# A product moved to the last step of each seven-product unit, and three products given a PSUM bank of their own, in a two-layer decoder kernel

## The chip, the cores and the metric

The kernel runs on one core of one Trainium2 chip. The metric is the device time of one execution in microseconds (us), lower is better. Below, PE is TensorE (matmuls), ACT is ScalarE, DVE is VectorE, POOL is GpSimd and SP is SyncE; SP and POOL issue the DMA transfers.

## The reference

A trunk of two layers on a sequence of 256 tokens with 2048 channels, all in float32. Layer 0 has differential attention, layer 1 latent attention, and each is followed by a SwiGLU feed-forward network (FFN). The change lies in the two FFNs alone:

```python
def _swiglu(h, w_in, w_out):
    g, u = jnp.split(h @ w_in, [FFN_HIDDEN], axis=-1)
    return (jax.nn.silu(g) * u) @ w_out

# in each layer i, FFN_HIDDEN = 5632
y = _swiglu(_rmsnorm(x, g[2]), ffn_w_in[i], ffn_w_out[i])
x = x + _rmsnorm(y, g[3])
```

## The kernel before

**Split matmuls.** Every float32 operand is split into a high and a low part (`split_to`: ACT makes the high part by a cast, L105, then DVE the low part by a subtraction, L106). A product of two such operands is three matmuls (`mm3`, L100 to L102). A piece of weights is 128 x 4 x 512 numbers, 1 MB. It comes by DMA into a staging buffer (`wst`, 2 buffers, or `wr`, 3 buffers) and is split in two halves into `whi` and `wlo`, which hold 6 halves each, three pieces. A product of one piece with one block of tokens is 12 matmuls of 512 columns.

**Blocks.** The hidden width is worked through in 11 blocks of 512 (`blk` 0 to 10). A block's input part makes the gate (m = 0) and the up half (m = 1) for the two blocks of 128 tokens (t = 0, 1) in four sums of the pool `mm` (4 PSUM banks). Odd blocks and blocks 0 and 10 do it in the plain way (`block_in`, 8 pieces of 24 matmuls). Blocks 2, 4, 6 and 8, the even blocks here, do half of it by seven products in place of eight, after Strassen and Winograd (`block_in_sevens`): seven products of 12 matmuls and four plain pieces of 24.

**Units.** The output part of two finished blocks is made by `unit`, again by seven products, from four pieces of `wout`. While an odd block from 3 on is worked on, two units run between its pieces, and block 10 has one: 9 units in each FFN. A unit's sums are in the pool `wp` (2 banks); each product's share is added to `y` in SBUF by `gather` (DVE, L716; or ACT, L713, where nothing is there yet).

**The right factors.** The seven right factors of a unit or an even block are sums of four weight pieces b11, b12, b21, b22, made in place in the three `wr` buffers by `right_factors`. Before, step k splits: 0 b11; 1 b21; 2 b11 + b12; 3 b22; 4 b11 + b12 + b22; 5 b12 + b22, the third sum; 6 the sum of all four. Two sums are made by DMAs that POOL issues and that add b12 from DRAM to a buffer: L690, after step 0's split, for step 2; and L694, after step 3's split and after the DVE addition L693, for step 5. The other two are DVE additions, L693 (for step 4) and L696 (for step 6).

**The even block's banks.** In `block_in_sevens` the bank `a` (the gate's sum for t = 1) holds step 0, then steps 4 and 5 on top of it, then step 6 and two plain pieces. Step 2 is alone in a `wp` bank (`lone`). DVE reads `a` after steps 4 (L600) and 5 (L604).

**Order.** Dependences, buffers and the order on each engine come from a planner that simulates the program; each engine then runs its list in that order, and so do the DMA queues' issuers SP and POOL. After block 8, `x_again` (L790) has POOL load the kept residual, 2 MB, into the buffer that the even blocks' left factors (`S`) held till then.

Of the kernel before, what the change touches and what calls it, by code (L numbers as in the profile page):

```python
# [9 lines left out]
F32 = mybir.dt.float32  # L10
# [4 lines left out]
ALU = mybir.AluOpType  # L15
AX = mybir.AxisListType

P = 128
SEQ = 256
NT = SEQ // P  # L20
D = 2048
KC = D // P
CW = 512
# [16 lines left out]
def trunk_kernel(ctx: ExitStack, tc: tile.TileContext, a: dict):  # L40
    nc = tc.nc
# [10 lines left out]
    sb = ctx.enter_context(tc.tile_pool(name="sb", bufs=2))  # L52
# [20 lines left out]
    def load_split(src, shape, loads=1, parts=1):  # L73

        w = wst.tile([P] + shape, F32, tag="w", name="w")
        n = shape[0] // loads
        for i in range(loads):
            nc.sync.dma_start(w[:, i * n : (i + 1) * n], src[:, i * n : (i + 1) * n])  # L80
        return split_weight(w, shape, parts)

    def split_weight(w, shape, parts=1):
        both = []
        half = shape[0] // 2
        for h in range(2):
            hi = whi.tile([P, half] + shape[1:], F32R, tag="whi", name="whi")
            lo = wlo.tile([P, half] + shape[1:], F32R, tag="wlo", name="wlo")
            n = half // parts
            for i in range(parts):  # L90
                c = slice(i * n, (i + 1) * n)
                split_to(hi[:, c], lo[:, c], w[:, h * half + i * n : h * half + (i + 1) * n])
            both += [(hi[:, i], lo[:, i]) for i in range(half)]
        return both
# [232 lines left out]
    def x_piece(ps, piece, kcs, t, first=None, more=False):  # L327
        first = kcs[0] == 0 if first is None else first
        for k, kc in enumerate(kcs):
            ts_ = slice(t * P, (t + 1) * P)  # L330
            mm3(ps, (xTh[:, kc, ts_], xTl[:, kc, ts_]), piece[k], first and k == 0, kc == KC - 1, more)
# [131 lines left out]
    def ffn(i, rstd, second_tokens, first_tokens, aside=None):  # L463
        win, wout = a[f"win{i}"], a[f"wout{i}"]
# [5 lines left out]
        def activation(g, u, hidden):  # L470
            hs = []
            for t in range(NT):
                sg = sb.tile([P, CW], F32, tag="t2k", bufs=4, name="sg")
                nc.scalar.activation(sg, g(t), AF.Silu, scale=rows[t])
                h = sb.tile([P, CW], F32, tag="t2k", bufs=4, name="h")
                nc.vector.scalar_tensor_tensor(h, u(t), rows[t], sg, op0=ALU.mult, op1=ALU.mult)
                hs.append(h)
            for t in (1, 0):
                pt = tr.tile([P, CW], F32, tag="tr", name="pt")
                for j in range(4):  # L480
                    nc.tensor.transpose(pt[:, j * P : (j + 1) * P], hs[t][:, j * P : (j + 1) * P], ident)
                hidden(t, pt.rearrange("p (k t) -> p k t", k=4))
# [26 lines left out]
        I = {}  # L509
# [56 lines left out]
        def block_in_sevens(blk, hidden):  # L566

            ps = {k: mm.tile([P, CW], F32, tag="mm", name="ps") for k in ((0, 1), (1, 0), (1, 1), (0, 0))}
            G = {k: gp.tile([P, CW], F32, tag="g", name="G") for k in ("11", "12", "22")}
            lone = wp.tile([P, CW], F32, tag="wp", name="lone")  # L570
            begun = set()

            def plain(m, pc, t, piece=None):
                piece = load_split(win[blk, m, pc], [4, CW]) if piece is None else piece
                x_piece(ps[m, t], piece, range(pc * 4, pc * 4 + 4), t, (m, t) not in begun, True)
                begun.add((m, t))
                return piece

            right = right_factors(win[blk, 0, 0], win[blk, 1, 0], win[blk, 0, 1], win[blk, 1, 1])

            def step(k, left, out, key=None):
                product(out, I[left], right(k), more=key in begun or k in (4, 5))
                if key:
                    begun.add(key)

            a, c = ps[0, 1], ps[1, 0]
            right(None)
            yield
            step(0, "A11", a, (0, 1))
            nc.scalar.copy(G["11"], a)  # L590
            u2 = plain(1, 2, 0)
            plain(1, 2, 1, u2)
            step(1, "A12", ps[0, 0], (0, 0))
            step(2, "-S1", lone)
            nc.scalar.copy(G["22"], lone)
            u3 = plain(1, 3, 0)
            plain(1, 3, 1, u3)
            step(3, "-S4", c, (1, 0))
            step(4, "S2", a)
            nc.vector.tensor_tensor(G["12"], G["22"], a, op=ALU.subtract)  # L600
            nc.vector.tensor_tensor(G["12"], c, G["12"], op=ALU.add)
            g2 = plain(0, 2, 0)
            step(5, "S3", a)
            nc.vector.tensor_tensor(G["22"], G["22"], a, op=ALU.subtract)  # L604
            nc.vector.tensor_tensor(G["22"], ps[1, 1], G["22"], op=ALU.add)
            g3 = plain(0, 3, 0)
            nc.vector.tensor_tensor(G["11"], ps[0, 0], G["11"], op=ALU.add)
            plain(0, 2, 1, g2)
            step(6, "A22", a, (0, 1))
            plain(0, 3, 1, g3)  # L610
            yield
            activation(lambda t: a if t else G["11"], lambda t: G["22"] if t else G["12"], hidden)

        def parts(name):
            both = mid.tile([P, 2, 2, 4, P], F32R, tag="mid", name=name)
# [53 lines left out]
        def product(ps, lhs, rhs, more=False):  # L669

            for k in range(4):
                mm3(ps, (lhs[0][:, k], lhs[1][:, k]), rhs[k], not more and k == 0, k == 3, more)

        def right_factors(b11, b12, b21, b22):

            w = {}

            def raw(src):
                t = wr.tile([P, 4, CW], F32, tag="r", name="wr")
                nc.sync.dma_start(t, src)  # L680
                return t

            def right(k):
                if k is None:
                    w["t"] = raw(b11)
                    w["b21"] = raw(b21)
                    return
                now = split_weight(w[("t", "b21", "t", "b22", "t", "b22", "t")[k]], [4, CW])
                if k == 0:
                    nc.gpsimd.dma_start(w["t"], b12, accum_op=ALU.add)  # L690
                    w["b22"] = raw(b22)
                elif k == 3:
                    nc.vector.tensor_tensor(w["t"], w["t"], w["b22"], op=ALU.add)  # L693
                    nc.gpsimd.dma_start(w["b22"], b12, accum_op=ALU.add)  # L694
                elif k == 4:
                    nc.vector.tensor_tensor(w["t"], w["t"], w["b21"], op=ALU.add)  # L696
                return now

            return right

        def unit(pair, X, cgs, first):

            (b1, b2), (n1, n2) = pair, cgs

            def sums():
                return wp.tile([P, CW], F32, tag="wp", name="wp")

            def ys(t, cg):
                return y[:, t, cg * CW : (cg + 1) * CW]

            def gather(t, cg, ps, sign, fresh=False):
                if fresh:
                    nc.scalar.mul(ys(t, cg), ps, sign)  # L713
                else:
                    op = ALU.add if sign > 0 else ALU.subtract
                    nc.vector.tensor_tensor(ys(t, cg), ys(t, cg), ps, op=op)  # L716

            right = right_factors(wout[b1, n1], wout[b1, n2], wout[b2, n1], wout[b2, n2])
            right(None)
            yield  # L720
            for k, left in enumerate(("A11", "A12", "S1", "S4", "S2", "S3", "A22")):
                if k == 0:
                    pa = sums()
                elif k in (1, 2):
                    pc = sums()
                ps, more = (pc, k == 3) if k in (1, 2, 3) else (pa, k > 0)
                product(ps, X[left], right(k), more)
                if k == 0:
                    gather(0, n1, ps, 1.0, first)
                elif k == 1:  # L730
                    gather(0, n1, ps, 1.0)
                elif k == 2:
                    gather(1, n2, ps, -1.0, first)
                elif k == 3:
                    gather(0, n2, ps, -1.0, first)
                elif k == 4:
                    gather(0, n2, ps, -1.0)
                elif k == 5:
                    gather(1, n2, ps, -1.0)
                else:  # L740
                    gather(1, n1, ps, 1.0, first)
                yield

        def chained(units):
# [49 lines left out]
        for blk in range(NBLK):  # L794
            if blk == NBLK - 1:
                A, hidden = single_operands()
                plain = plain_unit(pair, X, (2, 3))
# [392 lines left out]
```

## Time and profile before

| | |
|---|---|
| time, median of 3 runs | 2116.52 us (2114.79 to 2123.14) |
| the profiled execution | 2125.41 us, of which the span of the profile is 2123.6 us |
| busy in the span | PE 2066.8 us (97%), DVE 1606.5 (76%), ACT 1160.7 (55%), POOL 90.3 |
| granted clock of TensorE | 0.991 of full speed, mean over the span |

All times in the profile are microseconds from the first instruction unless marked ns. The ends of matmuls are modelled, so that a row's duration (0.39 us for 512 columns) is longer than the distance of two starts.

### The profile page before, as it was taken

Reading aid. Unit: us, or ns where it says so; the run is one execution under the profiler, and the core shown is the slowest. Engines: PE = TensorE matmul, PEld = TensorE weight load, DVE = VectorE, ACT = ScalarE, POOL = GpSimd, SP = SyncE. Lnnn points to the kernel's source line nnn. Section 1 sums busy time; section 2 is a strip of 40 time slices with the busy share of each in tenths; the row PEclk is TensorE's granted clock in tenths of the full one; section 3 lists DMA queues with packets and bytes.
Section 4 is the critical chain, followed back from the end, with each engine's and each line's share of the span. In section 5 each row is a group of like instructions: output and inputs, shape, how many; then the busy total and the mean of one; then the engine's idle time right before and its main releaser. Section 6 shows DMA issues by size and latency. Waiting matters only on the chain.

```text
span 2123.6 us, 26407 instructions
## 1 busy us (share of the span) xinstructions
PE 2066.8 (97%) x10278; PEld 1756.8 (83%) x10278; DVE 1606.5 (76%) x1851; ACT 1160.7 (55%) x1509; POOL 90.3 (4%) x139
## 2 busy tenths in 40 slices
PE   8999999999999999999998999999999999999997
PEld 7999998788887878878888898878777887878886
DVE  6655655777888888978777876486888888888866
ACT  6444444555665555646545654465655665556543
POOL 0000000000000000000001100000000000000000
PEclk9999999999999999999999999999999999999999
DMA  7554546466767767688644534466677776778752
GB/s 264 198 179 159 175 163 225 160 234 186 226 203 212 254 209 236 185 256 269 199 164 162 201 117 164 139 240 215 179 210 235 230 217 195 245 227 255 225 196 104
DMA packets 63772, 430.62 MB, mean 203 GB/s; under 512 B 7584, under 2 KB 7840, under 8 KB 14112
## 3 DMA queue, kind: packets, MB, share of 16 engines
q1 hardware_dynamic: 55584, 366.03, 47.2%
q0 software_dynamic: 8064, 62.92, 15.2%
q8 instruction: 80, 1.31, 0.2%
q14 instruction: 44, 0.36, 0.0%
HBM read 422.63 MB, written 6.29 MB: 202 GB/s over the span
## 4 chain that ended last, share of the span: by engine, by line
PE 75%; DVE 9%; DMA 8%; issue 6%; ACT 2%; POOL 0%; SPq 0%; ACTq 0%; POOLq 0%; DVEq 0%
PE ps L100 20%; PE ps L101 20%; PE ps L102 20%; DVE wlo L106 5%; DMA wr<-in_win 5%; PE wp L102 4%; PE wp L101 4%; PE wp L100 4%; DMA wr<-in_wout 2%; ACT whi L105 2%; DVE wr L693 1%; DVE x L260 1%; PE ps_s L1049 0%; PE ps_s L388 0%; PE ps_s L1050 0%
## 5 line engine op out<-in xcount | busy, mean ns | idle before, releaser
L106 DVE TENSOR_TENSOR wlo<-w,whi 128x1024 fp32r<-128x1024 f32 (+3 forms) x534 | 637.7, 1203 | 253.6 <-ACT whi L105 244.4
L105 ACT CAST whi<-w 128x1024 fp32r<-128x1024 f32 (+3 forms) x534 | 546.7, 1034 | 441.6 <-PE ps L102 255.9
L100 PE MATMUL ps<-whi,xTh 128*128 128x512 f32 (+2 forms) x1472 | 566.4, 391 | 19.9 <-ACT whi L105 16.6
L101 PE MATMUL ps<-wlo,xTh 128*128 128x512 f32 (+2 forms) x1472 | 570.0, 388 | 3.5 <-DVE wlo L106 3.4
L102 PE MATMUL ps<-whi,xTl 128*128 128x512 f32 (+2 forms) x1472 | 566.8, 387 | 1.4 <-DVE xTl L106 1.4
L106 DVE TENSOR_TENSOR wlo<-wr,whi 128x1024 fp32r<-128x1024 f32 x364 | 436.1, 1219 | 155.6 <-ACT whi L105 152.8
L105 ACT CAST whi<-wr 128x1024 fp32r<-128x1024 f32 x364 | 374.8, 1049 | 311.7 <-PE ps L102 107.2
L100 PEld LDWEIGHTS ps<-whi,xTh 128*128 128x128 f32 x1472 | 277.5, 189 | 78.3 <-ACT whi L105 20.5
L101 PEld LDWEIGHTS ps<-wlo,xTh 128*128 128x128 f32 x1472 | 278.1, 189 | 59.0 <-DVE wlo L106 6.5
L102 PEld LDWEIGHTS ps<-whi,xTl 128*128 128x128 f32 x1472 | 278.0, 189 | 55.5 <-DVE xTl L106 1.7
L100 PE MATMUL ps<-xTh,whi 128*128 128x256 f32 x512 | 146.3, 287 | 0.0
L102 PE MATMUL ps<-xTh,wlo 128*128 128x256 f32 x512 | 144.9, 283 | 0.2 <-DVE wlo L106 0.2
L101 PE MATMUL ps<-xTl,whi 128*128 128x256 f32 x512 | 144.7, 283 | 0.0
L100 PE MATMUL ps<-whi,oTh 128*128 128x512 f32 x256 | 100.7, 393 | 0.0
L101 PE MATMUL ps<-wlo,oTh 128*128 128x512 f32 x256 | 100.0, 391 | 0.0
L102 PE MATMUL ps<-whi,oTl 128*128 128x512 f32 x256 | 99.9, 390 | 0.0
L102 PEld LDWEIGHTS ps<-xTh,wlo 128*128 128x128 f32 x512 | 98.2, 192 | 0.5 <-DVE wlo L106 0.4
L101 PEld LDWEIGHTS ps<-xTl,whi 128*128 128x128 f32 x512 | 98.2, 192 | 0.3
L100 PEld LDWEIGHTS ps<-xTh,whi 128*128 128x128 f32 x512 | 98.1, 192 | 0.3
L716 DVE TENSOR_TENSOR y<-y,wp 128x512 f32<-128x512 f32 x110 | 74.8, 680 | 6.1 <-PE wp L102 5.8
L696 DVE TENSOR_TENSOR wr<-wr 128x2048 f32<-128x2048 f32 x26 | 59.4, 2285 | 0.3
L693 DVE TENSOR_TENSOR wr<-wr 128x2048 f32<-128x2048 f32 x26 | 59.4, 2284 | 0.1
(276 smaller groups left out, 2785.9 us busy)
## 6 DMA issues: line engine op xcount, KB each, us to landing
w<-in_win SPq DMA_DIRECT2D x144, 1024.0 KB, 5.7
wr<-in_wout SPq DMA_DIRECT2D x54, 1024.0 KB, 5.6
wr<-in_wout POOLq DMA_DIRECT2D x36, 1024.0 KB, 8.8
w<-in_wqk SPq DMA_DIRECT2D x32, 1024.0 KB, 4.8
w<-in_wo SPq DMA_DIRECT2D x32, 1024.0 KB, 4.9
wr<-in_win SPq DMA_DIRECT2D x24, 1024.0 KB, 6.9
wr<-in_win POOLq DMA_DIRECT2D x16, 1024.0 KB, 8.4
w<-in_wout SPq DMA_DIRECT2D x16, 1024.0 KB, 4.9
```

The source lines that it names most:

```text
L100: nc.tensor.matmul(out, lh, rh, start=first, stop=False, skip_group_check=more)
L101: nc.tensor.matmul(out, lh, rl, start=False, stop=False, skip_group_check=more)
L102: nc.tensor.matmul(out, ll, rh, start=False, stop=last, skip_group_check=more)
L105: nc.scalar.copy(hi, src)
L106: nc.vector.tensor_tensor(lo, src, hi.bitcast(F32), op=ALU.subtract)
L260: nc.vector.scalar_tensor_tensor(xs, y[:, t, cg * CW : (cg + 1) * CW], ry, xs, op0=ALU.mult, op1=ALU.add)
L693: nc.vector.tensor_tensor(w["t"], w["t"], w["b22"], op=ALU.add)
L696: nc.vector.tensor_tensor(w["t"], w["t"], w["b21"], op=ALU.add)
L716: nc.vector.tensor_tensor(ys(t, cg), ys(t, cg), ps, op=op)
```

## The change

Steps 5 and 6 are exchanged in each unit and in each even block: the sum of all four weight pieces is now split for step 5 and multiplied with A22, and the third sum, b12 + b22, that L694's DMA makes, is split for step 6 and multiplied with S3. In an even block, steps 0, 4 and 6 go to a second `wp` bank, `chain`, and `ps[0, 1]` holds the plain pieces and step 5 alone; since the gate's sum for t = 1 is then in two banks, ACT copies `chain` to SBUF (`sums`) and DVE adds `ps[0, 1]`. Plain pieces are no longer divided over two places, and the second follows step 3. In a unit, step 5 has a `wp` bank to itself, and step 6 joins steps 0 and 4, from where it is added to two places of `y`: one more `gather` a unit.

```diff
@@ -567,49 +567,49 @@
 
             ps = {k: mm.tile([P, CW], F32, tag="mm", name="ps") for k in ((0, 1), (1, 0), (1, 1), (0, 0))}
             G = {k: gp.tile([P, CW], F32, tag="g", name="G") for k in ("11", "12", "22")}
-            lone = wp.tile([P, CW], F32, tag="wp", name="lone")
+            lone, chain = (wp.tile([P, CW], F32, tag="wp", name=k) for k in ("lone", "chain"))
             begun = set()
 
-            def plain(m, pc, t, piece=None):
-                piece = load_split(win[blk, m, pc], [4, CW]) if piece is None else piece
-                x_piece(ps[m, t], piece, range(pc * 4, pc * 4 + 4), t, (m, t) not in begun, True)
-                begun.add((m, t))
-                return piece
+            def plain(m, pc):
+                piece = load_split(win[blk, m, pc], [4, CW])
+                for t in range(NT):
+                    x_piece(ps[m, t], piece, range(pc * 4, pc * 4 + 4), t, (m, t) not in begun, True)
+                    begun.add((m, t))
 
             right = right_factors(win[blk, 0, 0], win[blk, 1, 0], win[blk, 0, 1], win[blk, 1, 1])
 
-            def step(k, left, out, key=None):
-                product(out, I[left], right(k), more=key in begun or k in (4, 5))
-                if key:
-                    begun.add(key)
-
-            a, c = ps[0, 1], ps[1, 0]
+            def step(k, left, out):
+
+                if isinstance(out, tuple):
+                    product(ps[out], I[left], right(k), out in begun)
+                    begun.add(out)
+                else:
+                    product(out, I[left], right(k), k in (4, 6))
+
             right(None)
             yield
-            step(0, "A11", a, (0, 1))
-            nc.scalar.copy(G["11"], a)
-            u2 = plain(1, 2, 0)
-            plain(1, 2, 1, u2)
-            step(1, "A12", ps[0, 0], (0, 0))
+            step(0, "A11", chain)
+            nc.scalar.copy(G["11"], chain)
+            plain(1, 2)
+            step(1, "A12", (0, 0))
             step(2, "-S1", lone)
             nc.scalar.copy(G["22"], lone)
-            u3 = plain(1, 3, 0)
-            plain(1, 3, 1, u3)
-            step(3, "-S4", c, (1, 0))
-            step(4, "S2", a)
-            nc.vector.tensor_tensor(G["12"], G["22"], a, op=ALU.subtract)
-            nc.vector.tensor_tensor(G["12"], c, G["12"], op=ALU.add)
-            g2 = plain(0, 2, 0)
-            step(5, "S3", a)
-            nc.vector.tensor_tensor(G["22"], G["22"], a, op=ALU.subtract)
+            step(3, "-S4", (1, 0))
+            plain(1, 3)
+            step(4, "S2", chain)
+            nc.vector.tensor_tensor(G["12"], G["22"], chain, op=ALU.subtract)
+            nc.vector.tensor_tensor(G["12"], ps[1, 0], G["12"], op=ALU.add)
             nc.vector.tensor_tensor(G["22"], ps[1, 1], G["22"], op=ALU.add)
-            g3 = plain(0, 3, 0)
+            plain(0, 2)
+            step(5, "A22", (0, 1))
+            plain(0, 3)
             nc.vector.tensor_tensor(G["11"], ps[0, 0], G["11"], op=ALU.add)
-            plain(0, 2, 1, g2)
-            step(6, "A22", a, (0, 1))
-            plain(0, 3, 1, g3)
+            step(6, "S3", chain)
+            nc.scalar.copy(sums := sb.tile([P, CW], F32, tag="t2k", bufs=4, name="sums"), chain)
+            nc.vector.tensor_tensor(G["22"], G["22"], chain, op=ALU.subtract)
+            nc.vector.tensor_tensor(sums, ps[0, 1], sums, op=ALU.add)
             yield
-            activation(lambda t: a if t else G["11"], lambda t: G["22"] if t else G["12"], hidden)
+            activation(lambda t: sums if t else G["11"], lambda t: G["22"] if t else G["12"], hidden)
 
         def parts(name):
             both = mid.tile([P, 2, 2, 4, P], F32R, tag="mid", name=name)
@@ -685,7 +685,7 @@
                     w["t"] = raw(b11)
                     w["b21"] = raw(b21)
                     return
-                now = split_weight(w[("t", "b21", "t", "b22", "t", "b22", "t")[k]], [4, CW])
+                now = split_weight(w[("t", "b21", "t", "b22", "t", "t", "b22")[k]], [4, CW])
                 if k == 0:
                     nc.gpsimd.dma_start(w["t"], b12, accum_op=ALU.add)
                     w["b22"] = raw(b22)
@@ -718,12 +718,12 @@
             right = right_factors(wout[b1, n1], wout[b1, n2], wout[b2, n1], wout[b2, n2])
             right(None)
             yield
-            for k, left in enumerate(("A11", "A12", "S1", "S4", "S2", "S3", "A22")):
+            for k, left in enumerate(("A11", "A12", "S1", "S4", "S2", "A22", "S3")):
                 if k == 0:
                     pa = sums()
-                elif k in (1, 2):
+                elif k in (1, 2, 5):
                     pc = sums()
-                ps, more = (pc, k == 3) if k in (1, 2, 3) else (pa, k > 0)
+                ps, more = (pc, k == 3) if k in (1, 2, 3, 5) else (pa, k > 0)
                 product(ps, X[left], right(k), more)
                 if k == 0:
                     gather(0, n1, ps, 1.0, first)
@@ -736,9 +736,10 @@
                 elif k == 4:
                     gather(0, n2, ps, -1.0)
                 elif k == 5:
+                    gather(1, n1, ps, 1.0, first)
+                else:
                     gather(1, n2, ps, -1.0)
-                else:
-                    gather(1, n1, ps, 1.0, first)
+                    gather(1, n1, ps, 1.0)
                 yield
 
         def chained(units):
```

## Rows read from the trace of the kernel before

**Rows 1.** Waits of PE: engine, line, releaser: us in total, times, longest.
```profile
PE ps L100 <- ACT whi L105: 16.6, 9, 3.2
...
PE ps L100 <- DVE G L600: 3.6, 6, 0.6
```

**Rows 2.** Line L694: who waited for it (us, times), and its time to landing.
```profile
  ACT whi L105: 91.6, 16
...
DMA to landing us min/median/max: 7.9/8.5/10.8
```

**Rows 3.** Timeline of POOL, block 8, layer 0: start, us, instruction [idle before <-releaser].
```profile
898.74 0.86 POOL L694 DMA_DIRECT2D wr<-in_win  x1 [20.45 <-DVE wlo L106]
916.02 0.57 POOL L790 DMA_DIRECT2D x<-x_kept  x1 [16.43 <-PE ps L102]
924.06 0.85 POOL L690 DMA_DIRECT2D wr<-in_wout  x1 [7.46 <-DVE wlo L106]
```

**Rows 4.** Timeline of ACT, same block.
```profile
906.96 1.99 ACT L105 CAST whi<-wr 128x1024 fp32r<-128x1024 f32 x2 [6.21 <-DMA wr<-in_win]
908.86 1.99 ACT L105 CAST whi<-w 128x1024 fp32r<-128x1024 f32 x2
```

**Rows 5.** Timeline of PE, same block.
```profile
885.62 0.39 PE L102 MATMUL wp<-whi,A_A 128*128 128x512 f32 x1
...
909.95 0.51 PE L100 MATMUL ps<-whi,xTh 128*128 128x512 f32 x1 [2.18 <-ACT whi L105]
911.05 0.77 PE L100 MATMUL ps<-whi,S 128*128 128x512 f32 x1 [0.60 <-DVE G L600]
```

**Rows 6.** Windows, eight stalls, one quiet: busy PE, PEld, DVE, ACT, POOL; PEclk.
```profile
521.00:535.00 14.00, 12.54 (x54) 9.69 (x54) 11.10 (x13) 8.04 (x9) 0.00 (x0) 1.00 0.82 300
647.00:661.00 14.00, 12.14 (x53) 9.49 (x52) 10.01 (x12) 7.05 (x8) 0.00 (x0) 1.00 0.93 329
774.00:788.00 14.00, 11.17 (x42) 8.55 (x41) 10.03 (x11) 5.99 (x6) 0.00 (x0) 0.88 0.95 338
904.00:918.00 14.00, 11.22 (x42) 8.60 (x41) 9.82 (x11) 5.99 (x6) 0.57 (x1) 0.88 1.00 346
1508.00:1522.00 14.00, 12.47 (x54) 9.69 (x53) 10.99 (x13) 7.98 (x9) 0.00 (x0) 1.00 0.81 301
1637.00:1651.00 14.00, 11.05 (x48) 8.61 (x47) 9.94 (x11) 6.42 (x7) 0.00 (x0) 1.00 0.86 318
1765.00:1779.00 14.00, 10.99 (x41) 8.40 (x40) 9.54 (x11) 5.99 (x6) 0.00 (x0) 0.88 0.87 320
1896.00:1910.00 14.00, 10.25 (x32) 7.63 (x31) 9.38 (x10) 5.98 (x6) 0.57 (x1) 0.76 0.92 334
985.50:999.50 14.00, 14.00 (x63) 11.59 (x62) 12.51 (x11) 8.60 (x9) 0.84 (x1) 1.00 0.86 244
```

**Rows 7.** Windows around the four stalls in odd blocks, 10 us each, their sum.
```profile
sum 40.00, PE 35.52 PEld 27.82 DVE 32.93 ACT 29.55 POOL 0.00; mean PE 8.88 PEld 6.95 DVE 8.23 ACT 7.39 POOL 0.00
```

**Rows 8.** Groups by line: xcount | busy us, mean ns of one | idle before, releaser.
```profile
L716 DVE TENSOR_TENSOR y<-y,wp 128x512 f32<-128x512 f32 x110 | 74.8, 680 | 6.1 <-PE wp L102 5.8
...
L590 ACT COPY G<-ps 128x512 f32<-128x512 f32 x8 | 4.7, 590 | 0.6 <-PE ps L102 0.6
```

**Rows 9.** Windows: block 8 of layer 0 (even), then block 9 (odd).
```profile
878.60:926.20 47.60, 44.82 (x194) 36.54 (x193) 40.27 (x42) 27.21 (x31) 2.28 (x3) 0.96 0.78 247
926.20:1007.00 80.80, 79.83 (x357) 65.86 (x356) 69.18 (x65) 46.80 (x50) 2.56 (x3) 1.00 0.78 239
```

**Rows 10.** Timeline of DVE, same block.
```profile
888.57 0.68 DVE L716 TENSOR_TENSOR y<-y,wp 128x512 f32<-128x512 f32 x1
...
901.66 2.28 DVE L696 TENSOR_TENSOR wr<-wr 128x2048 f32<-128x2048 f32 x1
```

**Rows 11.** Line L690: who waited for it (us, times), and its time to landing.
```profile
  ACT whi L105: 48.5, 14
...
DMA to landing us min/median/max: 8.1/8.8/11.1
```

## The prediction, made before the changed kernel ran

> **What bounds the kernel now.** TensorE does: PE is busy for 97% of the span, so the question is what makes it wait, and what of that this change touches. I read the waits of PE first. Leaving the starts of the layers aside, what ends its idle time in the FFNs is a high part that ACT has yet to cast, and in the even blocks the DVE read L600 [rows 1]. Next come those who wait for the DMA of L694, the addition that makes the third sum: ACT, 16 times of 26, for 91.6 us in all, because that DMA needs 7.9 to 10.8 us to land [rows 2].
>
> The timelines of one block show how the first leads to the second. In block 8 of layer 0, POOL issues L694 at 898.74 [rows 3]. ACT's next work in its list is the cast of that sum (step 5, S3). It stands idle for 6.21 us until the DMA has landed at 906.9, and the cast of a plain piece, which needs nothing of that DMA, stands behind it in ACT's list and starts only at 908.86 [rows 4]. PE has by then used up what was split, and idles for 2.18 us before the plain piece and 0.60 us before S3's product, which overwrites the bank that DVE reads late in L600 [rows 5]. The granted clock falls as well: 0.88 in that window [rows 6], so some matmuls after the gap run at the lower of the two levels.
>
> What this costs in all is read from windows of 14 us around the stalls. An undisturbed one touches 63 matmuls of 512 columns, so one is worth 14 / 63 = 0.222 us. The eight even blocks' windows have 54, 53, 42, 42, 54, 48, 41 and 32: 9 + 10 + 21 + 21 + 9 + 15 + 22 + 31 = 138 matmuls fewer, 138 x 0.222 = 30.7 us [rows 6], the lower clock included. Four smaller stalls in odd blocks begin the same way (ACT waits for L694's landing, then a plain cast comes late); there PE is idle for 40 - 35.5 = 4.5 us [rows 7]. Together 35.2 us, 1.7% of the time.
>
> **The change, part by part.**
>
> *Steps 5 and 6 exchanged.* The cast that needs L694's DMA moves behind more work. In an even block PE has, between step 3's product and the cast's turn before, step 4's product and one half piece: 12 + 12 matmuls, 5.3 us. Afterwards it is piece (1, 3), step 4, piece (0, 2), step 5 and piece (0, 3): 24 + 12 + 24 + 12 + 24 = 96 matmuls, 21.3 us. Splitting runs at most three pieces ahead of PE, here at most (24 + 12 + 24) x 0.222 = 13.3 us, but both ends of that distance run ahead alike, so the slowest landing seen, 10.8 us [rows 2], fits. In the units step 5, and mostly a plain piece, are added to what covers it. So I take all 35.2 us as removed; the bounds are nothing (see the second rival) and 35.2.
>
> *Step 5 now needs L696.* That is a DVE addition of 2.28 us, which already stands right behind step 4's split: in block 8 it ended at 903.9 [rows 10], 3 us before the DMA landed. The new step 5 also has piece (0, 2) ahead of it, 24 x 0.222 = 5.3 us of PE. Cost nothing; without that cover up to 2.3 us for each of the 26 units and even blocks.
>
> *The bank of its own and the added reads.* The 0.6 us wait for L600 goes, since 60 matmuls now stand between steps 4 and 6; it is in the 35.2 already. Added are one gather in each of 18 units (0.68 us) and one DVE addition in each of 8 even blocks (0.68, as the other additions there), 26 x 0.68 = 17.7 us of DVE, and 8 ACT copies of 0.59, 4.7 us [rows 8]. What hides them is idle time of DVE: block 9 has 80.8 - 69.2 = 11.6 us for 1.4 us more; block 8 has 47.6 - 40.3 = 7.3 us [rows 9], of which the removed stall takes some 4.7 (21 matmuls), so 2.6 us are left for 0.7. The cover in the even blocks is thin but holds. I take nothing; with no cover at all it would be 17.7 + 4.7 = 22.4 us. The last step's copy and addition end an even block, where PE goes on with the next unit's first product.
>
> *What is late next.* L690's DMA is as slow, 8.1 to 11.1 us, and ACT waits for it too, 48.5 us in all [rows 11], but no stall of PE begins there today. From landing, step 2 needs a cast of 1.05 and a subtraction of 1.22 us: 8.8 + 2.3 = 11.1 us from the issue. In an even block the cover is step 0, a piece and step 1, 48 matmuls or 10.7 us, plus the distance by which the split leads. Before, the last product of the previous unit lay in between too (it ended at 886.0 in block 8 [rows 5]); afterwards it probably comes earlier, as it no longer waits for a gather. I put 0.5 us on each of 8 blocks, 4 us, bounds 0 and 2.7 (those 12 matmuls) x 8 = 21.
>
> *A queue that the moved step passes.* S3's product is the last reader of the even blocks' operands, and in block 8 POOL's L790 waits for it: issued at 916.0, with the next unit's L690 behind it at 924.1 [rows 3]. Now S3 ends with the block, some 10 us later. If the planner leaves L790 in front, L690 is held up, and 2 MB travel ahead of its own; if not, L790 is merely late, and nobody waits for it until the FFN's end. I take 1 us in each layer, 2 us; bounds 0 and 8 us each, the lead of L790 over L690 (924.06 - 916.02 [rows 3]), if all of it is lost.
>
> **The sum.** 35.2 - 4 - 2 = 29.2 us less: 2125.4 becomes 2096. The profiled execution is 8.9 us above the median of 2116.5. If these 8.9 us are stalls of the same sort (landings differ from run to run), the changed kernel's median is about 2096 too; if not, 2116.5 - 29.2 = 2087. Between the two I take **2091 us**.
>
> **Rivals.**
>
> 1. *The next wait takes half.* The bounds above for L690 and L790 come true in good part: 12 to 20 us given back (of 21 + 16), so 2116.5 - 35.2 + 12 to 20 = 2093 to 2101, and up to 2112 if L690's stalls lower the clock as L694's do. For it: ACT's 48.5 us of waiting [rows 11]. Against: PE has not one stall behind L690 now. Chance 0.17, centre 2103.
>
> 2. *The change does not do what it says.* The planner put a cast whose data landed at 906.9 in front of one that needs nothing of that DMA, so it seems to take the DMA to be faster than it is. It may again pull the sum's cast forward, whenever ACT is free and step 5 waits for L696; ACT would then stand at the same landing. Or the DMA lands sooner where no profile is taken: some 2.8 us sooner (2.18 + 0.60, PE's idle time in block 8 [rows 5]) leaves nothing to remove. Either way the time stays near 2116. Against: the split ran in the program's order in block 8, and not one landing was under 7.9 us [rows 2]. Chance 0.13.
>
>    A page of the Trainium skill says so much: "DMA: Bandwidth & Descriptors", section "Anatomy of one DMA — SWDGE (gpsimd) path", fits a DMA of this kind as about 2.0 us and its bytes over 436 GB/s, 4.4 us for 1 MB by my estimate from it, and by that there would be no stall here. The trace disagrees.
>
> 3. *Slower: two banks for three users.* `chain` takes the second `wp` bank, which the units use. An even block's first product must now wait until a unit's last sums are gathered: in block 8 the unit's last product ended at 886.0, but its gather ran from 888.57 to 889.25 [rows 5, 10], 3.2 us, and 3.9 with the second gather. At the even block's end the next unit's second product waits for the copy and subtraction of `chain`, about 0.8 us beyond the 2.7 us of the first product. With 4.7 us in each of 8 places, 38 us, plus 15 us for the clock (block 8's 2.8 us idle cost 4.7, so 1.9 each), the time is 2116.5 - 35.2 + 53 = 2134. It decides from 35.2 / 8 = 4.4 us per place on. Against: the planner knows DVE's list and can put the plain piece first, and the even block's bank can be that of step 5, which is gathered a product earlier. Chance 0.08.
>
> **How the numbers follow.** My forecast has 0.62, with a range of its own of 2080 to 2102. What a measurement of this kernel can tell from no change is about 0.5%, 10.6 us: the borders are 2106 and 2127. Faster: 0.62 and all but a little of the first rival, 0.78. Same: the second rival and that little, 0.14. Slower: 0.08. For 8 in 10 the range takes the forecast (0.62), the first rival (0.17) and a corner of the second: 2076, where both the 8.9 us and some relief in DVE's waits are gained, to 2112.
>
> **What the profile will show.** Right, if ACT's waits for L694 (91.6 us) fall to a fifth or less, if no window of an even block has fewer than 60 matmuls in 14 us where the S3 product was late, if the row for L600 among PE's waits is gone, and if PE's share is 98% or more with a clock near 0.995. Wrong in the next-wait way, if L690 stands in front of PE's idle time, in block 9 above all; in the second way, if casts of `wr` still wait 5 us and more behind L694; in the third, if PE waits for L716, or for reads of `chain`, where even blocks begin and end.

## The result, and the profile after

The changed kernel takes 2088.12 us (median of 4 runs, 2087.38 to 2089.11), the kernel before beside it 2118.07 (2114.79 to 2123.14). The ratio is 0.9857, 95% interval 0.9835 to 0.9878: 1.4% faster. The forecast was 2091 us, "faster" with 0.78. The profiled execution took 2089.11 us, 36.3 us less than the one before (2125.41); the spans differ by the same 36.3. By the medians of these runs it is 30.0 us.

The head of the page of the changed kernel:

```profile
span 2087.3 us, 26435 instructions
...
PE 2053.6 (98%) x10278; PEld 1751.2 (84%) x10278; DVE 1618.1 (78%) x1877; ACT 1162.0 (56%) x1517; POOL 90.8 (4%) x139
```

Its waits of PE (as before: us in total, times, longest), as [rows 1]:

```profile
PE pt L112 <- DMA x<-in_x: 5.7, 3, 3.9
PE pt L112 <- issue: 4.3, 1, 4.3
PE ps L100 <- ACT h L105: 2.5, 2, 1.2
...
PE chain L100 <- ACT whi L105: 0.2, 1, 0.2
```

PE's idle time fell from 2123.6 - 2066.8 = 56.8 us to 2087.3 - 2053.6 = 33.7, by 23.1. The same 10278 matmuls were also busy for 13.2 us less, with a mean granted clock of 0.995 in place of 0.991. Together that is the 36.3. What PE still waits for lies at the starts of attention and of the FFNs and at the FFNs' ends. In the blocks between, the high parts of weights (16.6 us before) are down to one wait of 0.2, and the row of L600 is gone.

The four signs that the prediction named are all there. Nobody waits for L694 any more (91.6 us before), although the DMA is as slow as it was. This is line L694, as [rows 2]:

```profile
who waited for it (us, times):
busy tenths in 40 slices 0000000000000000000000000000000000000000
DMA to landing us min/median/max: 7.7/8.6/9.7
```

The eight even blocks' windows of 14 us, as [rows 6], each where step 5 and what follows it runs (here two of layer 0, the emptiest, and the sum):

```profile
634.00:648.00 14.00, 13.92 (x62) 11.09 (x61) 13.94 (x12) 6.55 (x9) 0.86 (x1) 1.00 0.59 153
...
892.00:906.00 14.00, 14.00 (x63) 11.58 (x63) 13.50 (x14) 8.00 (x8) 0.00 (x0) 1.00 0.96 344
...
1605.00:1619.00 14.00, 13.77 (x60) 10.86 (x59) 13.94 (x12) 6.54 (x9) 0.87 (x1) 1.00 0.60 157
...
sum 112.00, PE 111.69 PEld 91.26 DVE 108.15 ACT 58.29 POOL 4.62; mean PE 13.96 PEld 11.41 DVE 13.52 ACT 7.29 POOL 0.58
```

The counts are 63, 62, 64, 63, 64, 60, 63 and 63 where they were 54 down to 32, all at a clock of 1.00. DVE is busy for 108 of these 112 us: in these stretches almost nothing is left of the idle time that was to hide the added reads. S3's product now comes at a block's end, behind such a window; block 8 of layer 0 and then block 9 as a whole, as [rows 9], leave PE no gap either:

```profile
867.00:911.50 44.50, 44.50 (x202) 36.95 (x201) 40.79 (x42) 27.60 (x32) 2.62 (x3) 1.00 0.74 227
911.50:993.00 81.50, 81.50 (x364) 67.41 (x364) 73.50 (x72) 49.12 (x53) 3.17 (x4) 1.00 0.82 265
```

Block 8 of layer 0 shows how the order came out. The timeline of ACT, as [rows 4]:

```profile
895.53 2.00 ACT L105 CAST whi<-wr 128x1024 fp32r<-128x1024 f32 x2 [6.46 <-DVE wr L696]
897.43 1.99 ACT L105 CAST whi<-w 128x1024 fp32r<-128x1024 f32 x2
899.55 1.05 ACT L105 CAST whi<-wr 128x1024 fp32r<-128x1024 f32 x1
900.92 1.05 ACT L105 CAST whi<-wr 128x1024 fp32r<-128x1024 f32 x1 [0.32 <-PE ps L102]
```

The timeline of POOL, as [rows 3]:

```profile
885.61 0.88 POOL L694 DMA_DIRECT2D wr<-in_win  x1 [16.96 <-DVE wlo L106]
907.39 0.86 POOL L690 DMA_DIRECT2D wr<-in_wout  x1 [20.90 <-DVE wlo L106]
912.08 0.56 POOL L791 DMA_DIRECT2D x<-x_kept  x1 [3.83 <-PE chain L102]
```

The timeline of PE, first two matmuls of S3's product, as [rows 5]:

```profile
903.84 0.39 PE L100 MATMUL chain<-whi,S 128*128 128x512 f32 x1
...
909.06 0.39 PE L101 MATMUL chain<-wlo,S 128*128 128x512 f32 x1
```

L694 is issued at 885.61 and, by the median of 8.6 us, lands near 894. The third sum's two half casts come at 899.55 and 900.92, well after that. ACT still stands for 6.46 us in this block, but for L696, and PE has split pieces to work on meanwhile. The planner let L690 (907.39) go ahead of the residual's load (912.08, now L791), the reverse of [rows 3]. And it pulled the first matmul of S3's product 5.2 us ahead of the rest, to 903.84.

### The profile page after: what moved, and what is told of

Its sections match the earlier page's. It is cut to its first block, busy times and chain, and to the rows that moved or that the text cites. A ratio compares the mean times of both kernels' runs of the same rounds, so it can differ in the third digit from the quotient of the medians.

```text
span 2087.3 us, 26435 instructions
## 1 busy us (share of the span) xinstructions
PE 2053.6 (98%) x10278; PEld 1751.2 (84%) x10278; DVE 1618.1 (78%) x1877; ACT 1162.0 (56%) x1517; POOL 90.8 (4%) x139
## 4 chain that ended last, share of the span: by engine, by line
PE 87%; DVE 6%; issue 3%; DMA 3%; ACT 1%; SPq 0%; POOL 0%; DVEq 0%; POOLq 0%; ACTq 0%
PE ps L101 22%; PE ps L102 22%; PE ps L100 22%; PE wp L100 5%; PE wp L102 5%; PE wp L101 5%; DVE wlo L106 3%; DMA wr<-in_win 2%; PE chain L101 1%; PE chain L102 1%; PE chain L100 1%; DVE x L260 1%; PE pt L481 1%; DMA wr<-in_wout 1%; ACT whi L105 1%
## 5 line engine op out<-in xcount | busy, mean ns | idle before, releaser
L101 PE MATMUL ps<-wlo,xTh 128*128 128x512 f32 (+2 forms) x1440 | 556.0, 388 | 0.1
L102 PE MATMUL ps<-whi,xTl 128*128 128x512 f32 (+2 forms) x1440 | 553.6, 386 | 1.4 <-DVE xTl L106 1.4
L100 PE MATMUL ps<-whi,xTh 128*128 128x512 f32 (+2 forms) x1440 | 547.1, 390 | 2.2 <-DVE y L281 1.5
L100 PEld LDWEIGHTS ps<-whi,xTh 128*128 128x128 f32 x1440 | 271.1, 189 | 55.0 <-ACT xTh L105 3.1
L102 PEld LDWEIGHTS ps<-whi,xTl 128*128 128x128 f32 x1440 | 271.7, 189 | 54.1 <-DVE xTl L106 1.7
L101 PEld LDWEIGHTS ps<-wlo,xTh 128*128 128x128 f32 x1440 | 271.8, 189 | 52.6 <-DVE wlo L106 1.0
L716 DVE TENSOR_TENSOR y<-y,wp 128x512 f32<-128x512 f32 x128 | 85.6, 681 | 2.2 <-PE wp L102 2.2
L696 DVE TENSOR_TENSOR wr<-wr 128x2048 f32<-128x2048 f32 x26 | 59.5, 2289 | 0.3
```

The costliest lines, as they stand in the source:

```text
L100: nc.tensor.matmul(out, lh, rh, start=first, stop=False, skip_group_check=more)
L101: nc.tensor.matmul(out, lh, rl, start=False, stop=False, skip_group_check=more)
L102: nc.tensor.matmul(out, ll, rh, start=False, stop=last, skip_group_check=more)
```

## The experiments

Each set ran on one chip, beside runs of the kernel before on it; rows with the same time of before are one set, and the changed kernel itself was run again in the second set alone. Medians in us:

| kernel | time | before, same chip | ratio (95%) |
|---|---|---|---|
| exchange in the units alone | 2127.25 | 2124.53 | 1.0018 (1.0008 to 1.0028) |
| change in the even blocks alone | 2088.44 | 2124.53 | 0.9829 (0.9814 to 0.9844) |
| even blocks: bank alone, no exchange | 2106.31 | 2124.53 | 0.9914 (0.9899 to 0.9928) |
| before, without L694 | 2098.95 | 2124.53 | 0.9879 (0.9862 to 0.9895) |
| changed kernel again | 2088.36 | 2118.44 | 0.9858 (0.9841 to 0.9874) |
| bank alone, without L694 | 2095.19 | 2118.44 | 0.9890 (0.9875 to 0.9905) |
| before, with L694 twice | 2369.94 | 2118.44 | 1.1192 (1.1170 to 1.1213) |
| changed, with L694 twice | 2237.12 | 2118.44 | 1.0556 (1.0540 to 1.0572) |
| changed, without L694 | 2088.50 | 2126.46 | 0.9824 (0.9809 to 0.9838) |
| changed, without the added reads | 2089.57 | 2126.46 | 0.9826 (0.9810 to 0.9842) |
| bank alone, no L694, residual later | 2095.60 | 2126.46 | 0.9856 (0.9841 to 0.9871) |
| bank alone, residual later | 2107.51 | 2126.46 | 0.9913 (0.9898 to 0.9928) |

**Units or even blocks?** The change done in one place at a time.

```diff
 # units alone: in unit() and in the order of the right factors as in the change
-            for k, left in enumerate(("A11", "A12", "S1", "S4", "S2", "S3", "A22")):
+            for k, left in enumerate(("A11", "A12", "S1", "S4", "S2", "A22", "S3")):
 # even blocks alone: block_in_sevens as in the change, unit() as before
```

> Steps 5 and 6 exchanged in the units alone; the even blocks are as in the kernel before. If the gain comes from giving L694's DMA more time (first theory), the four stalls in odd blocks go and the eight in even blocks stay: 4 to 6 us less than before, 2112 to 2114. If it comes from the even blocks' own bank and undivided pieces (second theory), nothing changes: 2118.

> The even blocks as in the changed kernel, the units as before. First theory: the eight large stalls go and those in odd blocks stay: 24 to 31 us less than before, 2087 to 2094, and ACT still waits for L694 in the units. Second theory: all of the gain, 2088. The two lie close here; the run shows with the one before it whether the two parts add up to the whole.

The even blocks alone give 36.1 us, all of the gain; the units alone give nothing (2.7 us more than before). That is the time that the second theory had for the units, though the stalls that the first theory spoke of did go. With the units alone, ACT's waits for L694 fall from 16 to 8, and what is left is all in the even blocks; the four stalls of [rows 7] are gone. But small new ones stand where an odd block passes into an even one, or ends. The sum of six such windows, in which PE is idle for 36 - 31.58 = 4.4 us and DVE is busy throughout:

```profile
sum 36.00, PE 31.58 PEld 24.16 DVE 36.00 ACT 27.64 POOL 1.68; mean PE 5.26 PEld 4.03 DVE 6.00 ACT 4.61 POOL 0.28
```

With the even blocks alone, ACT still waits for L694 (who waited for that line), yet PE's waits hold a single 0.6 us for a weight's high part:

```profile
  ACT whi L105: 32.9, 8
```

So the units' waits cost nothing once the even blocks are changed, without the exchange in the units. Why is not shown; with another order in the even blocks, the planner's lists differ elsewhere too.

**The wait for the DMA, or the shared bank?** In the even blocks the change does two things: it puts L694's sum last, and it gives three products a bank of their own, with undivided plain pieces. The second was tried alone, with the third sum still at step 5; in place of the first, the DMA was taken out of the kernel before.

```diff
 # bank alone (step 5 still S3, pieces undivided, (1, 3) ahead of step 3); lines shortened
+            plain(0, 2)
+            step(5, "S3", chain)
+            nc.scalar.copy(sums, chain)
+            plain(0, 3)
+            step(6, "A22", (0, 1))
 # before, without L694
-                    nc.gpsimd.dma_start(w["b22"], b12, accum_op=ALU.add)
```

> The even blocks get the bank of their own, the copy and the added sum and undivided pieces, but S3 stays step 5 and A22 step 6, as before; the units are as before. Second theory: nearly all of the gain, 2088 to 2092. First theory: the cover of L694's DMA grows only by the half piece that is no longer put off, 12 matmuls or 2.7 us, so stalls of 2.7 us and more keep their rest and those in odd blocks stay: 2094 to 2104, with ACT still waiting for L694 in the even blocks, 3 us and more each time.

> The kernel before without L694's DMA: the third sum lacks b12, 26 MB fewer are moved, all else stays. First theory: all stalls go with the wait, 30 to 38 us less than before, 2080 to 2088. Second theory: the bank and the divided pieces still hold PE up, 2110 or more.

Neither half gives it all, and neither time lies in a range expected: the bank alone came out above both of its ranges, and the kernel without the DMA between its two. The exchange itself in the even blocks, without a bank of their own, was not run. Without the DMA the kernel before gains 25.6 us, against the 35.2 that I had put to the DMA. Something else then stands in the even blocks. PE's waits there:

```profile
PE ps L100 <- DVE G L604: 4.0, 8, 0.5
PE ps L101 <- DVE wlo L106: 3.7, 7, 1.4
```

and the same eight stretches' windows, the first, the last, and their sum:

```profile
525.00:539.00 14.00, 13.50 (x60) 10.83 (x59) 11.16 (x14) 7.13 (x8) 0.86 (x1) 1.00 0.75 291
...
1878.00:1892.00 14.00, 12.10 (x52) 9.42 (x51) 11.91 (x14) 6.45 (x7) 1.04 (x2) 1.00 1.00 407
sum 112.00, PE 105.08 PEld 82.73 DVE 93.20 ACT 56.22 POOL 7.45; mean PE 13.13 PEld 10.34 DVE 11.65 ACT 7.03 POOL 0.93
```

They touch 60, 58, 57, 56, 60, 58, 57 and 52 matmuls, 458 in place of 8 x 63 = 504. Those 46 x 0.222 us are 10.2 us, and 2098.95 - 2088.44 = 10.5 us is what this kernel lacks to the even-blocks version on the same chip. In all eight blocks PE's next product into the bank waits until DVE has read it in L604, a wait that in the kernel before stood in the list twice, for 1.0 us. The row of L600 is gone without the DMA. So the wait for the DMA had made PE wait for L600 and had hidden most of the waits for L604. Of the 10.2 us these waits name 4.0. Another 3.7 are late low parts of weights; whether they too come from the shared bank is not shown, and the rest no row names.

The bank alone gains 18.2 us, more than that 10.5. Its undivided piece (0, 2) also puts 12 + 24 matmuls in place of 12 + 12 in front of S3's product, 2.7 us more of cover for L694. ACT still waits for L694 78.7 us in 16 waits. The two halves overlap: 25.6 + 18.2 is more than the 36.1 of both.

**The bank alone, without the DMA.** If the two causes are all there is, this should reach the changed kernel.

> The run with the even blocks' bank of their own and S3 as step 5, now without L694's DMA (the third sum lacks b12). If the wait for the DMA (some 26 us) and the bank (some 10 us) are two separate causes that together make the gain: 2086 to 2090, as fast as the changed kernel. If one of them already holds all that is to be had, as fast as the better of the two alone: 2099.

It falls 6.8 us short of the changed kernel beside it (2095.19 against 2088.36), between the two values expected. The even blocks are clean: the windows of layer 0 touch 64, 63, 63 and 63 matmuls, those of layer 1 64, 64, 63 and 63. So the bank of its own, with its undivided pieces, does take away what was left there. What is missing now is in block 9 of both layers; four windows of 10 us there:

```profile
919.00:929.00 10.00, 8.67 (x41) 6.72 (x40) 5.20 (x4) 6.28 (x8) 0.00 (x0) 1.00 0.56 193
941.00:951.00 10.00, 8.60 (x38) 6.79 (x37) 10.00 (x11) 3.84 (x4) 0.00 (x0) 1.00 0.97 379
1892.00:1902.00 10.00, 7.91 (x39) 6.05 (x38) 4.61 (x4) 5.68 (x7) 0.00 (x0) 1.00 0.64 209
1915.00:1925.00 10.00, 8.60 (x38) 6.79 (x37) 9.87 (x11) 3.84 (x4) 0.00 (x0) 1.00 0.98 391
sum 40.00, PE 33.78 PEld 26.34 DVE 29.68 ACT 19.65 POOL 0.00; mean PE 8.45 PEld 6.59 DVE 7.42 ACT 4.91 POOL 0.00
```

PE is idle for 6.2 of these 40 us. In POOL's list the residual's load (here L789) stands directly in front of the first unit's L690, the order that the prediction feared (timeline of POOL):

```profile
906.61 0.56 POOL L789 DMA_DIRECT2D x<-x_kept  x1 [38.24 <-PE chain L102]
907.64 0.89 POOL L690 DMA_DIRECT2D wr<-in_wout  x1 [0.47 <-DVE wlo L106]
```

ACT's cast of that sum, in its timeline:

```profile
922.72 2.00 ACT L105 CAST whi<-wr 128x1024 fp32r<-128x1024 f32 x2 [9.49 <-DMA wr<-in_wout]
```

L690 is issued at 907.64, and ACT is released at 922.7, 15 us later. The second window of each layer has a stall of 1.4 us for a low part that DVE has yet to make. DVE had stood idle for 5.7 us until that late cast, and is then busy without a pause from 923.8 to 951, so this stall may well follow from the first. To see whether the load in front is the cause, its call was moved behind block 9 in the program, with and without L694:

```diff
-            if blk == NBLK - 3:
+            if blk == NBLK - 2:
                 x_again()
```

> As the run with the bank of its own, S3 as step 5 and no L694 (the third sum lacks b12), but the load of the kept residual is put behind block 9. In that run the load stood directly in front of block 9's L690, which took 15 us to land. If this is what kept it from the changed kernel's time: 6 to 8 us less, 2087 to 2090, with no stall of PE in block 9. If not: 2095.

> The run with the bank of its own and S3 as step 5 (with L694), the residual's load behind block 9. If the load's place costs by itself: 4 to 8 us less than 2106, 2098 to 2102. What is then left to 2088 is the wait for L694 with S3 as step 5.

Neither time moved (2095.60 after 2095.19, 2107.51 after 2106.31, from different sets), but neither did the order on the chip: the planner put the load in the same place of POOL's list, directly ahead of L690, 1.0 us without L694 and 5.6 with it, as before. So these two runs tell nothing. The traces at hand say more. This is block 9's first L690 in five kernels, layer 0 and layer 1:

| kernel | load issued ahead of L690, us | L690 from issue to landing, us |
|---|---|---|
| bank alone, without L694 | 1.0, 1.0 | 15.0, 15.7 |
| bank alone | 5.6, 5.6 | 12.6, 12.9 |
| before, without L694 | 7.1, 7.0 | 11.7, 11.6 |
| before | 8.0, 8.4 | 11.1, 9.6 |
| changed | 4.7 and 4.6 behind it | 10.9, 11.3 |

The nearer in front of it the load stands, the later L690 lands. The kernels differ in more than this distance, so that the load delays L690 is likely, but not shown.

**How much cover has L694 now?** The DMA taken out of the changed kernel, and the DMA issued twice, in the kernel before and in the changed one.

```diff
                     nc.gpsimd.dma_start(w["b22"], b12, accum_op=ALU.add)
+                    nc.gpsimd.dma_start(w["b22"], b12, accum_op=ALU.add)
```

> The changed kernel without L694's DMA (the third sum lacks b12, 26 MB fewer are moved). If the change hides that DMA wholly: 2086 to 2089, as fast as with it. If a part of its landing is still paid for: 2084 or less.

> The kernel before with L694's DMA issued twice in a row (the third sum has b12 twice, 26 MB more are moved), so that the sum lands some 8.5 us later. First theory: the wait is exposed, so most of it comes on top in each even block and a part in each unit: 60 to 180 us more than before. If the wait was hidden and the bank alone cost: within 10 us of before.

> The same second DMA in the changed kernel. First theory: two landings, 17 us, still fit into the 21.3 us of PE's work that I counted between step 3 and step 6 in an even block, and less well into a unit: 0 to 25 us above the changed kernel, far less than in the kernel before. If the exchange had not moved the cast behind enough work: as much more as in the kernel before.

Without the DMA the changed kernel takes 2088.50 us. With it, it took 2088.12 and 2088.36 in the other sets, so its cost is hidden. Moving 26 MB less thus gains nothing by itself, and the 25.6 us of the kernel before are likely the wait and not the traffic. Doubled, the DMA costs the kernel before 251 us, 9.7 in each of 26 places, and the changed kernel 2237.12 - 2088.36 = 149 us, 5.7 in each. In the changed kernel PE's idle time rose from 33.7 to 129.2 us, 3.7 in each place; the rest is longer busy time, at a mean clock of 0.974. I had expected 0 to 25 us, from a cover of 21.3 us and two landings of 8.5. Both numbers were off. The second DMA (L695) starts when the first has landed and took 13.0 us, so that the two take some 22. Who waited for it in the changed kernel, and its landings:

```profile
  ACT whi L105: 229.8, 24
...
DMA to landing us min/median/max: 12.2/13.0/14.0
```

The timeline of POOL at one unit:

```profile
895.31 0.88 POOL L694 DMA_DIRECT2D wr<-in_wout  x1 [18.03 <-DVE wlo L106]
904.45 0.86 POOL L695 DMA_DIRECT2D wr<-in_wout  x1 [8.26 <-DMA wr<-in_wout]
```

The cast of that sum on ACT:

```profile
917.27 1.99 ACT L105 CAST whi<-wr 128x1024 fp32r<-128x1024 f32 x2 [10.44 <-DMA wr<-in_wout]
```

The timeline of PE there, where S3's product begins:

```profile
918.36 0.79 PE L100 MATMUL wp<-whi,A_S 128*128 128x512 f32 x1 [2.42 <-ACT whi L105]
919.62 0.80 PE L101 MATMUL wp<-wlo,A_S 128*128 128x512 f32 x1 [0.47 <-DVE wlo L106]
```

The sum is there 917.3 - 895.3 = 22 us after L694's issue, and PE waits 2.42 + 0.47 us for its two parts, which leaves some 19 us of cover in this unit. For block 8 of the changed kernel the timeline above gives somewhat less: S3's first matmul runs at 903.84, 18.2 us after L694's issue, and needs the high part alone, so that with a half cast (1.05) ahead of it a landing may take some 17 us. The rest of the product starts 5.2 us later. My 21.3 was the time of 96 matmuls; it left out the cast and the planner's pulling of that first matmul ahead.

**The added reads.** The changed kernel without the units' second gather of step 6 and the even blocks' copy and addition:

```diff
 # lines shortened
-                    gather(1, n1, ps, 1.0)
-            nc.scalar.copy(sums, chain)
-            nc.vector.tensor_tensor(sums, ps[0, 1], sums, op=ALU.add)
```

> The changed kernel without what it added on DVE and ACT: the second gather of step 6 in each unit, the copy of the chain and the added sum in each even block (so the output and one gate sum lack those shares). If they are hidden, as I predicted: 2086 to 2089. If they are paid for, up to 22 us less, 2066.

It takes 2089.57 us: not faster than the changed kernel (2088.12 and 2088.36 in the other sets), though DVE's busy time falls from 1618.1 to 1605.8 us. The added reads cost nothing.

## Why the prediction was right, and where its working was not

- **The mechanism** is confirmed: with the DMA's landing behind more work, ACT's waits for L694, PE's idle time behind them and the fall of the clock, in four of the eight even blocks [rows 6], are gone, and removing the DMA then gains nothing more.
- **35.2 us removed** was the right total for the profiled executions (36.3 measured; 30.0 by the medians of that set, 36.1 for the even blocks alone in the first set of experiments), with the wrong split. The windows counted matmuls lost for any reason, and I put all of them to the DMA and, in passing, 0.6 us to L600. The DMA is worth 25.6 us. The other 10.5 us come out once the DMA no longer hides them, as waits for L604's reads of the shared bank and for late low parts, and they go with the bank of its own and the undivided pieces, which were not tried apart. Had the change only moved the sum, the forecast would, by the run without the DMA, have been too good. The step that failed is "in the 35.2 already", taken without asking what stands behind the first wait.
- **The units** entered with 4.5 us. The units' exchange alone removed those stalls, but 4.4 us of new ones came elsewhere; the even blocks' change without it gave the whole gain.
- **The cover** of 21.3 us in an even block was some 17, since a cast comes between landing and use and the planner pulled the first matmul of S3 ahead. It still holds the slowest landing of the changed kernel, 9.7 us.
- **L696 at no cost** holds: ACT waits for it 45.7 us in 11 waits, and PE not once.
- **L690 (4 us) and L790 (2 us)** did not come. ACT waits more for L690 (61.9 us in 18 waits, 48.5 in 14 before), but PE has no stall there, in block 9 of layer 0 not one gap. The planner put L690 ahead of the residual's load; the bank alone without L694 shows the other order, the two 1.0 us apart, with 6 us of idle PE. What two of the even blocks' windows still lack is 1 and 3 of 63 matmuls, 4 x 0.222 = 0.9 us, so even if that stood for these terms they were some 5 us too large.
- **The first rival** (the next wait takes half) did not come; the bank-alone versions, with POOL's other order, show what it might have looked like. **The second** came in the small: the planner did pull one matmul of S3 ahead, but no cast in front of the landing, and the landings were not short. By the Trainium skill, "DMA: Bandwidth & Descriptors", section "Anatomy of one DMA — SWDGE (gpsimd) path", 4.4 us was to be expected by my estimate; the 26 landings after, 7.7 to 9.7 us, disagree with it as those before did. **The third** shows nowhere: no wait of PE for a gather, or for reads of `chain`.
- **2087 or 2096** for the median turned on the 8.9 us between the profiled execution and the median of before. In the sets of runs here the kernel before took 2118.1 to 2126.5 us as a median, the changed kernel and the versions that equal it 2088.1 to 2089.6. So those microseconds go with the change, as the base of 2125.4 had it; that they were stalls of the same sort is likely, but the kernel before was profiled once, so no trace shows it. From that base, 29.2 us less gave 2096.2, and the measured 36.3 gives 2089.1: 1.1 us more was removed than the 35.2, and the 6 us were not given back. From the other, 2087 came close to the 2088.12 only because the low base and the short sum cancel. Choosing 2091, between the two bases, made up for most of the error by chance.

What stays open: whether the residual's load in front of L690 causes the 6 to 7 us in block 9 of the bank alone without L694, what the exchange would give in the even blocks without a bank of their own, and why the units' waits cost nothing once the even blocks are changed. No version was faster than the changed kernel; the even blocks alone, and the kernel without its third DMA, only equal it.

## What to carry to other kernels

A stall that is counted as lost matmuls in a window is right in its sum, but it names only the wait that ended last: before all of it is put to one cause, ask which wait would stand there next, since here 10 of 36 us were other waits, a bank's readers among them, that a late DMA hid. In engines that run a fixed list, a piece of work that depends on a slow transfer does harm through what is queued behind it, and moving it to the end of its unit cures that without making the transfer faster. Cover is to be counted from the issue to the first instruction that needs the data, in the order that the engine really has, less what comes between landing and use, and not as the work that stands between in the program.

## What the runs showed of the hardware

- An adding DMA of 1 MB issued as soon as another one into the same buffer had landed took 12.2 to 14.0 us to land in the changed kernel (10.2 to 13.7 in the kernel before), against 7.7 to 9.7 for the first. Why is not shown.
- L690, issued 1.0 us after a load of 2 MB, landed 15.0 and 15.7 us later; issued 5.6 us after it, 12.6 and 12.9; issued 7.0 and 7.1 us after it, 11.6 and 11.7. Its medians in these kernels are 8.4 to 8.7.
- The median of the kernel with stalls differed by 8 us between the sets of runs, that of the versions without them by 1.5.
